# Interleaving two tensors: opening with one whole x tile and one whole y tile, in place of two halves of x

## The chip, the core and the metric

The kernel runs on one core of a Trainium2 chip. The metric is the device time of one execution in microseconds (us), as the median of several runs; smaller is better. Beside it stands the profile of one execution, taken by the hardware profiler, and its trace.

## What is computed

```python
def setup_inputs():
    batch, seq, dim = 32, 256, 1024
    # x and y: float32 of shape (batch, seq, dim)
...
def reference(x, y):
    result = np.zeros((batch, seq, dim * 2), dtype=np.float32)
    result[..., 0::2] = x
    result[..., 1::2] = y
    return result
```

The output takes its even elements from x and its odd ones from y. Nothing is calculated: each of the 33.55 MB inputs is read once, and 67.11 MB are written.

## The kernel before

The inputs are treated as flat arrays and cut into n = 8 tiles of 128 partitions by W = 8192 float32, 4 MB each. A partition's row of a tile is 32 KiB, and contiguous in memory. One x tile and one y tile make two output tiles of the same size: output half h of step k holds columns h x 4096 to (h + 1) x 4096 of both.

There are two buffers each for x (`xt`), y (`yt`) and the output (`ot`); step k uses `xt[k % 2]` and `yt[k % 2]`, and half h always uses `ot[h]`. The order is written by hand, with semaphores:

- **SyncE** issues the loads, x before y in each step (L45, L48). From step 2 on it waits until the buffer has been read: for x on the third copy of step k - 2, for y on the fourth (L43, L47; `woven` counts copies, four in a step).
- **VectorE** does the copies, four in a step: x into the even elements of half 0 (L60), y into its odd elements (L63), then the same two for half 1. Ahead of half 0 it waits for the step's x tile and, between the two copies, for its y tile (L55, L62). Ahead of each x copy from step 1 on it waits until the store that last read this output buffer has landed (L59).
- **ScalarE** issues the stores: one for each half, after the y copy of that half (L67, L68).

The first tile of x is different. It is loaded as two halves of 128 x 4096 (rows of 16 KiB), the first on SyncE's queue (L37), the second on ScalarE's (L38), each with its own semaphore; VectorE waits for the second half only ahead of its second x copy (L57). In step 0 SyncE's loop then loads only y (L44 to L48). After the kernel is written, lines 88 to 107 take the first DMA of SyncE and the first of ScalarE out of the body and put them in the opening block of the program, ahead of that engine's drain; both must be free of waits.

The kernel ends when ScalarE has seen the last stores of both halves land (L72 to L78).

Of the kernel before, what the change touches and what calls it, by code (L numbers as in the profile page):

```python
# [3 lines left out]


def _interleave(nc, x, y, out):
    P = 128
    W = 8192
    H = W // 2  # L10

    total = 1
    for s in x.shape:
        total *= s
    n = total // (P * W)
    assert n * P * W == total

    def rows(ap, names, k):
        flat = ap.rearrange("b s d -> (b s d)")
        return flat[k * names : (k + 1) * names].rearrange("(p w) -> p w", p=P)  # L20

    fp32 = mybir.dt.float32
    xt = [nc.alloc_sbuf_tensor(f"xt{b}", [P, W], fp32).ap() for b in (0, 1)]
    yt = [nc.alloc_sbuf_tensor(f"yt{b}", [P, W], fp32).ap() for b in (0, 1)]
    ot = [nc.alloc_sbuf_tensor(f"ot{b}", [P, W], fp32).ap() for b in (0, 1)]

    xsem = [nc.alloc_semaphore(f"xsem{b}") for b in (0, 1)]
    hsem = nc.alloc_semaphore("hsem")
    ysem = [nc.alloc_semaphore(f"ysem{b}") for b in (0, 1)]
    woven = nc.alloc_semaphore("woven")  # L30
    osem = [nc.alloc_semaphore(f"osem{b}") for b in (0, 1)]

    xs = [rows(x, P * W, k) for k in range(n)]
    ys = [rows(y, P * W, k) for k in range(n)]
    os_ = [rows(out, 2 * P * W, k) for k in range(n)]

    nc.sync.dma_start(out=xt[0][:, :H], in_=xs[0][:, :H]).then_inc(xsem[0], 16)  # L37
    nc.scalar.dma_start(out=xt[0][:, H:], in_=xs[0][:, H:]).then_inc(hsem, 16)  # L38

    for k in range(n):  # L40
        b = k % 2
        if k >= 2:
            nc.sync.wait_ge(woven, 4 * (k - 2) + 3)  # L43
        if k:  # L44
            nc.sync.dma_start(out=xt[b], in_=xs[k]).then_inc(xsem[b], 16)  # L45
        if k >= 2:
            nc.sync.wait_ge(woven, 4 * (k - 2) + 4)  # L47
        nc.sync.dma_start(out=yt[b], in_=ys[k]).then_inc(ysem[b], 16)  # L48

    for k in range(n):  # L50
        b = k % 2
        for h in (0, 1):
            c = slice(h * H, (h + 1) * H)
            if h == 0:
                nc.vector.wait_ge(xsem[b], 16 * (k // 2 + 1))  # L55
            elif k == 0:
                nc.vector.wait_ge(hsem, 16)  # L57
            if k:
                nc.vector.wait_ge(osem[h], 16 * k)  # L59
            nc.vector.tensor_copy(out=ot[h][:, 0::2], in_=xt[b][:, c]).then_inc(woven, 1)  # L60
            if h == 0:
                nc.vector.wait_ge(ysem[b], 16 * (k // 2 + 1))  # L62
            nc.vector.tensor_copy(out=ot[h][:, 1::2], in_=yt[b][:, c]).then_inc(woven, 1)  # L63

    for k in range(n):
        for h in (0, 1):
            nc.scalar.wait_ge(woven, 4 * k + 2 * h + 2)  # L67
            nc.scalar.dma_start(  # L68
                out=os_[k][:, h * W : (h + 1) * W], in_=ot[h]
            ).then_inc(osem[h], 16)  # L70

    nc.scalar.wait_ge(osem[0], 16 * n)  # L72
    used = sorted(s.num for s in [*xsem, hsem, *ysem, woven, osem[0]])
    assert used == list(range(used[0], used[-1] + 1)), used
    nc.scalar.sem_clear(range(used[0], used[-1] + 1))
    nc.scalar.nop(nofuse=True).wait_op(osem[1], 16 * n, "sem-ge").then_inc(
        osem[1], -16 * n
    )  # L78


def kernel(tc, x, y, out):
    nc = tc.nc
    tc.close()
    tc.compile()

    _interleave(nc, x, y, out)

    blocks = nc.main_func.blocks
    for engine in (mybir.EngineType.SP, mybir.EngineType.Activation):
        opening = blocks[0].instructions  # L90
        at, moved = next(
            (b, i)
            for b in blocks[1:]
            for i in b.instructions
            if i.engine == engine and i.opcode == "DMACopy"
        )
        assert not (moved.sync_info and moved.sync_info.on_wait)
        body = at.instructions
        body.remove(moved)
        gate = next(  # L100
            n
            for n, i in enumerate(opening)
            if i.engine == engine and i.opcode == "Drain"
        )
        opening.insert(gate, moved)
        at.instructions = body
        blocks[0].instructions = opening


# [1 line left out]
_INS = ['x', 'y']  # L111
_OUTS = [((32, 256, 2048), 'float32')]


# [23 lines left out]
```

## Time and profile before

| | |
|---|---|
| time, median of 5 runs | 314.73 us (314.59 to 314.93) |
| profiled execution, its own time | 314.71 us |
| its span | 313.2 us |
| VectorE busy | 72.6 us (23%), 32 copies of 2.29 us |
| DMA | 134.22 MB, mean 429 GB/s over the span, 4752 packets |
| SyncE's queue (q1) | 2304 packets, 65.01 MB |
| ScalarE's queue (q10) | 2448 packets, 69.21 MB |

The span runs from the first instruction recorded to the last event; the time of the execution lies 1.5 us above it. Part 2 of the page cuts the span in 40 slices of 7.8 us: each digit is the busy share in tenths, and for DMA the mean share of the core's 16 DMA engines. The answers by stretch give the same for any stretch asked for; DMA bytes and times are booked in the stretch where a packet starts, so short stretches can stand above the true rate and their neighbours below it. Transfers "to landing" are timed from the instruction that issues them to the last increment of their semaphore; in a queue with other transfers ahead, that holds their time in the queue.

### The profile page before, as it was taken

The page shows a single profiled execution, that of the slowest core. Times are in us where ns is not written, and L with a number is a line of the kernel's source. Part 1 is how long each engine was busy: PE and PEld are TensorE (multiplying, and loading weights), DVE is VectorE, ACT ScalarE, POOL GpSimd, SP SyncE. Part 2 cuts the span into 40 slices and gives each one's busy share as a digit, 9 for nine tenths or more (in the row PEclk, how much of TensorE's full clock was granted, in tenths as well). Part 3 has the DMA queues.
Part 4 walks back from the last instruction along what each step waited for, and adds up shares of the span by engine and source line. Part 5 has one row for each costly group of instructions (what it writes and reads, how often), then busy time and mean ns, then how long its engine had stood idle before and what let it go on. Part 6 is the DMA issues. An engine that isn't in the chain of part 4 may idle for free.

```text
span 313.2 us, 113 instructions
## 1 busy us (share of the span) xinstructions
DVE 72.6 (23%) x32; POOL 0.2 (0%) x4
## 2 busy tenths in 40 slices
DVE  0216002232022410324003250031501315013510
POOL 0000000000000000000000000000000000000000
DMA  8999999999999999999999999999999999999998
GB/s 343 460 410 393 444 427 431 439 427 444 418 452 410 460 402 469 402 465 406 456 414 444 427 431 439 427 444 418 452 410 460 402 469 402 465 406 456 414 444 360
DMA packets 4752, 134.22 MB, mean 429 GB/s; under 512 B 528, under 2 KB 528, under 8 KB 528
## 3 DMA queue, kind: packets, MB, share of 16 engines
q10 hardware_dynamic: 2448, 69.21, 51.2%
q1 hardware_dynamic: 2304, 65.01, 48.6%
HBM read 67.11 MB, written 67.11 MB: 429 GB/s over the span
## 4 chain that ended last, share of the span: by engine, by line
DMA 82%; DVE 12%; issue 0%
DMA out_dram<-ot 76%; DMA yt<-in_y_dram 6%; DVE ot L63 6%; DVE ot L60 6%
## 5 line engine op out<-in xcount | busy, mean ns | idle before, releaser
L60 DVE COPY ot<-xt 128x4096 f32<-128x4096 f32 x16 | 36.7, 2295 | 183.0 <-DMA out_dram<-ot 171.4
L63 DVE COPY ot<-yt 128x4096 f32<-128x4096 f32 x16 | 36.7, 2292 | 42.7 <-DMA yt<-in_y_dram 42.7
L122 POOL MEMSET const-bfloat16-1.0<- 128x1 bf16 x1 | 0.1, 102 | 0.0
L122 POOL MEMSET const-uint8-127<- 128x1 uint8 x1 | 0.1, 101 | 0.0
L122 POOL MEMSET const-float32-0.0<- 128x1 f32 x1 | 0.1, 99 | 0.2 <-issue 0.2
L122 POOL MEMSET const-float32-1.0<- 128x1 f32 x1 | 0.1, 98 | 0.0
## 6 DMA issues: line engine op xcount, KB each, us to landing
out_dram<-ot ACTq DMA_DIRECT2D x16, 4096.0 KB, 29.1
yt<-in_y_dram SPq DMA_DIRECT2D x8, 4096.0 KB, 60.8
xt<-in_x_dram SPq DMA_DIRECT2D x7, 4096.0 KB, 43.6
xt<-in_x_dram SPq DMA_DIRECT2D x1, 2048.0 KB, 11.6
xt<-in_x_dram ACTq DMA_DIRECT2D x1, 2048.0 KB, 13.3
```

What stands on the lines that cost most here:

```text
L60: nc.vector.tensor_copy(out=ot[h][:, 0::2], in_=xt[b][:, c]).then_inc(woven, 1)
L63: nc.vector.tensor_copy(out=ot[h][:, 1::2], in_=yt[b][:, c]).then_inc(woven, 1)
L122: nc = _bacc.Bacc("TRN2", target_bir_lowering=False, num_devices=1)
```

## The change

The first x tile is loaded whole by SyncE, and the first y tile whole by ScalarE, both in rows of 32 KiB. SyncE's loop then issues nothing in step 0. The semaphore of the second half of x, and VectorE's wait for it, are gone.

```diff
@@ -25,7 +25,6 @@
     xsem = [nc.alloc_semaphore(f"xsem{b}") for b in (0, 1)]
-    hsem = nc.alloc_semaphore("hsem")
     ysem = [nc.alloc_semaphore(f"ysem{b}") for b in (0, 1)]
...
-    nc.sync.dma_start(out=xt[0][:, :H], in_=xs[0][:, :H]).then_inc(xsem[0], 16)
-    nc.scalar.dma_start(out=xt[0][:, H:], in_=xs[0][:, H:]).then_inc(hsem, 16)
+    nc.sync.dma_start(out=xt[0], in_=xs[0]).then_inc(xsem[0], 16)
+    nc.scalar.dma_start(out=yt[0], in_=ys[0]).then_inc(ysem[0], 16)
 
     for k in range(n):
         b = k % 2
...
             nc.sync.dma_start(out=xt[b], in_=xs[k]).then_inc(xsem[b], 16)
         if k >= 2:
             nc.sync.wait_ge(woven, 4 * (k - 2) + 4)
-        nc.sync.dma_start(out=yt[b], in_=ys[k]).then_inc(ysem[b], 16)
+        if k:
+            nc.sync.dma_start(out=yt[b], in_=ys[k]).then_inc(ysem[b], 16)
 
     for k in range(n):
         b = k % 2
...
             if h == 0:
                 nc.vector.wait_ge(xsem[b], 16 * (k // 2 + 1))
-            elif k == 0:
-                nc.vector.wait_ge(hsem, 16)
             if k:
                 nc.vector.wait_ge(osem[h], 16 * k)
...
-    used = sorted(s.num for s in [*xsem, hsem, *ysem, woven, osem[0]])
+    used = sorted(s.num for s in [*xsem, *ysem, woven, osem[0]])
```

The program's order of instructions changes on two engines. SyncE has the x tile 0, then the x and y tiles 1, then those of step 2 behind their waits; it had half of x tile 0, y tile 0, x and y tile 1. ScalarE opens with y tile 0 and goes on with the 16 stores as before. VectorE's 32 copies keep their order.

## The prediction

> **What bounds the kernel now.** I read the page first, part 2, for whether any engine is full.
>
> ```profile
> DVE  0216002232022410324003250031501315013510
> ...
> DMA  8999999999999999999999999999999999999998
> GB/s 343 460 410 393 444 427 431 439 427 444 418 452 410 460 402 469 402 465 406 456 414 444 427 431 439 427 444 418 452 410 460 402 469 402 465 406 456 414 444 360
> ```
>
> VectorE is idle for most of every slice; the DMA engines are at 9 from the second slice to the last but one. The GB/s row swings because a transfer is booked where it starts, so I asked for wider stretches, with the opening cut fine. The columns are the stretch, its length, busy time of VectorE and GpSimd, clock, DMA share, GB/s.
>
> ```profile
> 0.00:4.00 4.00, 0.00 (x0) 0.20 (x4) 1.00 0.79 266
> 4.00:24.00 20.00, 4.35 (x2) 0.00 (x0) 1.00 1.03 445
> 24.00:32.00 8.00, 4.65 (x3) 0.00 (x0) 1.00 0.99 381
> 32.00:152.00 120.00, 27.27 (x12) 0.00 (x0) 1.00 1.00 433
> 152.00:272.00 120.00, 27.26 (x12) 0.00 (x0) 1.00 1.00 433
> ```
>
> Both long stretches move 433 GB/s at a share of 1.00. That is the ceiling of this kernel: 134.22 MB (part 2) / 433 GB/s = 310.0 us of the 313.2 us span. About 3.2 us are left for everything else: the start, the end, and whatever is lost on the way. By this view 0 to 4 us loses (433 - 266) x 4 / 433 = 1.5 us and 24 to 32 us loses (433 - 381) x 8 / 433 = 0.96 us. Stretch 4 to 24 shows 445, above the ceiling, by the same booking; so these two losses may each be off by some tenths.
>
> The chain that ended last, in its first 68 us, says which instructions set the opening (start, length, what):
>
> ```profile
> 1.57 20.36 DMA yt<-in_y_dram
> 21.93 0.02 issue
> 21.95 2.29 DVE ot L63
> 24.25 2.21 DVE ot L60
> 26.45 2.21 DVE ot L63
> 28.66 0.02 issue
> 28.68 38.84 DMA out_dram<-ot
> ```
>
> The chain looks serial, but its DMA links are elastic: the store issued at 28.68 takes 38.84 us, a 4 MB tile that at 433 GB/s needs 9.7. It is queued behind the store before it, and shares the engines with loads. So a chain that begins later gets shorter waits, as long as both queues hold work. **The question is therefore not whether the first store is late, but whether the DMA engines go idle.**
>
> **The change, part by part.** The bytes stay (the same tiles, loaded once), and so do the 32 copies and 16 stores. One DMA goes (33 to 32): two 2 MB halves of x and a y tile become one x tile and one y tile. By the order of instructions, SyncE then has x0, x1, y1 ahead of its first wait, where it had half of x0, y0, x1, y1; ScalarE opens with y0 where it had the other half of x0.
>
> 1. When x0 and y0 land. The issues of before:
>
> ```profile
> yt<-in_y_dram SPq DMA_DIRECT2D x8, 4096.0 KB, 60.8
> ...
> xt<-in_x_dram SPq DMA_DIRECT2D x1, 2048.0 KB, 11.6
> xt<-in_x_dram ACTq DMA_DIRECT2D x1, 2048.0 KB, 13.3
> ```
>
> The two halves, issued at 0.00 and 0.12, land at 11.6 and 0.12 + 13.3 = 13.4: together, so the two queues share the engines in small turns. From 13.4 to y0's landing at 21.93 (chain) are 8.5 us, at 433 GB/s 3.68 MB of y0's 4.19; the other 0.51 MB came before ScalarE's half was through. That is one 32 KiB row on each of 16 engines (0.52 MB): SyncE's queue got one row of its next tile in ahead of the end of ScalarE's transfer. In after the same happens with x1's first row: y0 lands when x0, y0 and one row per engine of x1 have moved, 0.52 MB / 433 = **1.2 us later**, at 23.1. Before, x0's first half led by 13.4 - 11.6 = 1.8 us (a half row, 0.6, and a whole one, 1.2); now it is two whole rows, so x0 lands at about 23.1 - 2.4 = 20.7, not 11.6.
>
> The Trainium skill (DMA: Bandwidth & Descriptors, Queues, rings and completion order) has each engine drain a packet of some 9 to 17 descriptors from one ring before it turns to the next. An engine's share of one of these DMAs is about that long, so by the rule x0 would drain whole, then y0 would land at 21.9 as before, and this step would cost 0. The landings 11.6 and 13.4 speak for the finer turns, and I go by them.
>
> 2. VectorE. The first copy (L60, 2.29 us) ran from 11.63, far ahead. With x0 at 20.7 it ends at 23.0, still before y0 at 23.1. So the early copy stays hidden under y0's transfer, by only 0.1 us; were that cover gone, the first store would slip by up to 2.3 us more. The copies after it follow as before: 2.3 us to the first store, now issued at 25.5 instead of 24.28; the second at 29.9 instead of 28.7; SyncE's x2 and y2, which wait for the third and fourth copy, at 27.7 and 29.9 instead of 26.48 and 28.68. No wait is added; the one on the second half of x0 goes.
>
> 3. Do the engines run dry meanwhile? Behind x0, SyncE's queue holds x1 and y1, 8.39 MB, 19.4 us of transfer at 433 GB/s. From 23.1 they last alone until over 40 us, and x2 is there by 27.7. So the 1.2 us are filled with loads that have to be done anyway. Cost 0; without that cover it would be 1.2 us. VectorE's waits then take up the shift: its longest, 19.6 us for the first store's landing, shows the room.
>
> 4. The middle and the end. The loads are ahead of the stores by about 0.5 MB more, so they are through a little sooner and the stores run alone a little longer. From 286 us on only stores are under way:
>
> ```profile
> 280.54 2.29 DVE L60 COPY ot<-xt 128x4096 f32<-128x4096 f32 x1 [14.88 <-DMA out_dram<-ot]
> 287.80 2.30 DVE L63 COPY ot<-yt 128x4096 f32<-128x4096 f32 x1 [4.96 <-DMA yt<-in_y_dram]
> 293.85 2.29 DVE L60 COPY ot<-xt 128x4096 f32<-128x4096 f32 x1 [3.75 <-DMA out_dram<-ot]
> 296.06 2.29 DVE L63 COPY ot<-yt 128x4096 f32<-128x4096 f32 x1
> ```
>
> The last store is issued at 298.4; the one before it takes 9.7 us from 293.8, to 303.5. So ScalarE's queue has 5 us in hand, and this doesn't depend on the shift. Cost 0.
>
> 5. Rows of 32 KiB in the opening. In the trace's records of single DMA packets, which no part of the page prints, a row of 16 KiB takes 611 ns and one of 32 KiB 1213. Per engine 16 half rows go for 8 whole: 16 x 611 - 8 x 1213 = 72 ns, plus one semaphore record of 9 ns: -0.1 us.
>
> 6. The cold start. No row shows a first transfer of 32 KiB rows. The first 16 KiB rows took 1.0 to 1.4 us, 0.4 to 0.8 over the 611. If that excess is a latency it stays (0); if it grows with the row it doubles (+0.6). Below nothing: were the excess gone, -0.6, but the first read has to come from somewhere, so I see no way. I take 0, as second rows are mostly at 611 already.
>
> The Trainium skill (DMA: Bandwidth & Descriptors, Latency and other measured facts) speaks against streams at large power-of-two distances in HBM: 512 KiB between rows gave 207 GB/s. If two tensors read side by side counted as such, an estimate by that figure is 8.39 MB / 207 - 8.39 / 433 = +21 us. The rows here lie 32 KiB apart as before, and the 433 of before comes with loads and stores on different tensors together, so I give it nothing.
>
> 7. The dip at 24 to 32 us. It begins with the first store. Should it come from the first store itself, it only moves by 1.2 us: 0. Should it come from ScalarE's queue starting anew after 11 us of rest (13.4 to 24.3), it may shrink, since the rest is now 23.1 to 25.5: down to -0.96. The first reason is nearer, as ScalarE's first load at 0.12 shows no dip of its own; I take 0.
>
> Sum against the profiled run (314.71 us, 1.5 outside its span; the median shown is 314.73): 314.71 - 0.1 = **314.6 us**.
>
> **The rivals.**
> - The shift is handed on (slower). The first store is 1.2 us late, and the chain runs from it through 15 stores to the end. If anywhere behind it the engines idle for want of a store or a load, the delay comes out whole: 314.7 + 1.2 = 315.9. It decides from the point where one queue is empty while the other's next transfer is still waited for. For it: the chain itself, 76% in stores. Against it: 433 GB/s at a share of 1.00 over 240 us, so there is no idle time of the engines that a delay could enter.
> - The dip goes (faster). ScalarE's queue is nearly in steady use, and the 0.96 us at 24 to 32 are not lost: 314.6 - 0.96 = 313.6. For it: the dip comes when that queue starts again. Against it: the first store after loads is as new as before.
> - The order is not shared but whole tiles (the change then moves almost nothing on the way to the first store): x0 at 11.6, y0 at 21.9, 314.6 as well.
>
> **How the numbers follow.** Forecast, full DMA engines hide the shift: 0.74, 314.1 (half the dip) to 315.3 (step 6 at +0.6, rounded). Whole tiles in turn: 0.03. Handed on: 0.15. Dip gone: 0.08. About 0.2% (0.63 us) is what a measurement of this kernel can tell from no change: faster 0.08, same 0.77, slower 0.15. The range takes in the slower rival and leaves out the faster: 314.0 to 315.9, some 9 in 10 by these cases, cut for sizes I don't foresee.
>
> **What would show it.** Right: the first L60 copy starting near 20.7, the first L63 copy near 23.1, the first store near 25.5; 433 GB/s from 32 us on; a stretch of 24 to 32 still below 400; first stretch near 266; the end of the span 1.5 us under the time. Wrong: a DMA share under 0.98 in any long stretch from 32 us on, the first 4 us under 230 GB/s (cold rows cost more), or no dip.

## The result and the profile after

| | before | after |
|---|---|---|
| median | 314.72 us (44 runs, 314.5 to 315.23) | 315.04 us (26 runs, 314.83 to 315.41) |
| profiled execution | 314.71 us | 315.41 us, the highest of its runs |
| its span | 313.2 us | 313.9 us |

The ratio is 1.0011, 95% interval 1.0006 to 1.0017. So the change lies within the 0.2% that the prediction called the same, and within its range, but it is slower by a small amount that is clear of noise, where the forecast had a gain of 0.1 us. What has to be explained is small: 0.3 us in the median, 0.7 us between the two traces.

The issue of the first store before, and then the first copies and the first store of after, in order of time (start, length, what; in brackets what ended the idle time before it; the length of a store's line covers several issues):

```profile
24.28 4.77 ACTq L68 DMA_DIRECT2D out_dram<-ot  x2
```

```profile
21.88 2.30 DVE L58 COPY ot<-xt 128x4096 f32<-128x4096 f32 x1 [21.88 <-DMA xt<-in_x_dram]
24.08 2.29 DVE L61 COPY ot<-yt 128x4096 f32<-128x4096 f32 x1
26.29 2.29 DVE L58 COPY ot<-xt 128x4096 f32<-128x4096 f32 x1
26.41 48.74 ACTq L66 DMA_DIRECT2D out_dram<-ot  x4
```

x0 lands at 21.85, not at 11.6 as its first half did; y0 at 22.0 (21.9 from its issue at 0.12), practically where it was (21.93). The first x copy is no longer hidden under y0's transfer, and the first store is issued 2.13 us later than before (24.28). The stretches of after, by the same cuts (stretch, length, busy time of VectorE and GpSimd, clock, DMA share, GB/s):

```profile
0.00:4.00 4.00, 0.00 (x0) 0.20 (x4) 1.00 0.75 270
4.00:24.00 20.00, 2.12 (x1) 0.00 (x0) 1.00 1.03 444
24.00:32.00 8.00, 6.78 (x4) 0.00 (x0) 1.00 0.99 365
32.00:152.00 120.00, 27.07 (x12) 0.00 (x0) 1.00 1.00 433
152.00:272.00 120.00, 27.47 (x13) 0.00 (x0) 1.00 1.00 433
```

Only the third line has moved: 365 where it was 381. (433 - 365) x 8 / 433 = 1.26 us are lost there, 0.3 more than before. From 32 us on the engines move 433 GB/s, as before, although everything is issued later; what takes up the delay is VectorE's waits (engine, line, what it waited for, us in total, times, longest):

```profile
DVE ot L58 <- DMA out_dram<-ot: 192.6, 14, 20.1
...
DVE ot L61 <- DMA yt<-in_y_dram: 12.1, 7, 1.7
```

Before, the second of these rows was

```profile
DVE ot L63 <- DMA yt<-in_y_dram: 42.7, 8, 8.0
```

The loads are now further ahead of the stores, so y is waited for less and the stores more.

What the 0.3 us do at the end is seen in the last microsecond. A packet is booked where it starts, so a stretch near the end tells how many engines still start a 32 KiB row there. Before and after:

```profile
311.70:312.00 0.30, 0.00 (x0) 0.00 (x0) 1.00 0.00 0
312.00:313.00 1.00, 0.00 (x0) 0.00 (x0) 1.00 0.01 0
```

```profile
311.70:312.00 0.30, 0.00 (x0) 0.00 (x0) 1.00 1.01 437
312.00:313.00 1.00, 0.00 (x0) 0.00 (x0) 1.00 0.08 33
```

Before, no engine starts a row after 311.7 us. After, four start one by 312.0 (437 GB/s x 0.3 us = 131 KB), and one engine alone starts one later (33 KB, one row). The kernel waits for all sixteen increments of the last store's semaphore, one from each engine, so it ends when the last of the 16 engines does.

The records of single packets, which no view prints whole, give the rest; I followed each engine as a chain of packets without gaps. Beyond the plain 611 ns and 1213 ns of a row, the engines lose 0.83 us each on average between 20 and 48 us before, and 1.17 after, and nothing after 48 us in either. The last increment of the last store's semaphore comes at 312.84 before and 313.54 after: 0.70 us later, as the two times are (315.41 - 314.71 = 0.70). The times of last increments are counted, here and below, from a zero that lies about 0.34 us behind that of the views, where the two are at 313.18 and 313.88; all other times are those of the views. And in both kernels the loss is where the first store's rows join the loads: it covers the two load rows per engine ahead of the first store row. Below, this is called the **join**; its stall is the average per engine from these records, of one trace for each kernel.

### The profile page after: what moved, and what is told of

Its sections match the earlier page's. It is cut to its first block, busy times and chain, and to the rows that moved or that the text cites. A ratio compares the mean times of both kernels' runs of the same rounds, so it can differ in the third digit from the quotient of the medians.

```text
span 313.9 us, 112 instructions
## 1 busy us (share of the span) xinstructions
DVE 72.5 (23%) x32; POOL 0.2 (0%) x4
## 4 chain that ended last, share of the span: by engine, by line
DMA 82%; DVE 13%; issue 0%
DMA out_dram<-ot 75%; DMA xt<-in_x_dram 7%; DVE ot L58 7%; DVE ot L61 6%
## 6 DMA issues: line engine op xcount, KB each, us to landing
yt<-in_y_dram ACTq DMA_DIRECT2D x1, 4096.0 KB, 21.9
```

## The experiments

**The theories.** All loss is at the join. Theory 1: it is larger because the first store comes later. Rival 1: the opening costs it, by its 32 KiB rows or its queues. Rival 2: it is what ScalarE's queue pays for starting anew, or what the output's first write pays; then it could be avoided.

**before_hold.** Only the moment of the first store is changed, in the kernel before:

```diff
             if k:
                 nc.vector.wait_ge(osem[h], 16 * k)
+            elif h == 0:
+                nc.vector.wait_ge(ysem[0], 16)
             nc.vector.tensor_copy(out=ot[h][:, 0::2], ...)
```

> The kernel before, with one more wait: the first x copy waits for the first y tile, so that the four copies of step 0 run in a row and the first store is issued near 26.4 us, as in the changed kernel, while the opening's loads stay as they were. Theory (the loss is the stall of the DMA engines around the first store, and it grows because this store comes 2.1 us later): the stall grows from 0.83 us per engine to about 1.2, time 315.0. Rival (the opening's queues or rows cost it, not the store's moment): 314.7, stall 0.8.

Measured: first store issued at 26.69 us; 315.51 us median (315.05 to 320.22), ratio 1.004 (1.0015 to 1.0064). So the opening of before is slow too when its first store comes where the changed kernel has it. But eight of the twelve runs lie at 315.05 to 315.52 and four at 318.05 to 320.22, which nothing here explains and which lift the ratio above that of the medians. The trace is of one of the two fastest runs (315.05). Its average stall did not grow (0.64, where the theory wanted 1.2); its last increment came late all the same (313.18), on one engine. So the moment of the store is borne out, and the larger average stall is not.

**after_rows16.** The changed kernel in 16 KiB rows:

```diff
-    nc.sync.dma_start(out=xt[0], in_=xs[0]).then_inc(xsem[0], 16)
-    nc.scalar.dma_start(out=yt[0], in_=ys[0]).then_inc(ysem[0], 16)
+    for c in (slice(0, H), slice(H, W)):
+        nc.sync.dma_start(out=xt[0][:, c], in_=xs[0][:, c]).then_inc(xsem[0], 16)
+        nc.scalar.dma_start(out=yt[0][:, c], in_=ys[0][:, c]).then_inc(ysem[0], 16)
```

> The changed kernel with both opening tiles cut in two DMAs of 16 KiB rows each, VectorE waiting for both halves as it waits for the whole. Theory (the moment of the first store): 315.0, stall near 1.2 us per engine. Rival (rows of 32 KiB in the opening): back to 314.7, stall near 0.8.

Measured: 314.70 us, ratio 0.9998 (0.9989 to 1.0006), stall 0.77. That is what the rival said. But the first store was issued at 25.96 here, 0.45 us earlier than in the changed kernel, so the run had not changed the rows alone. Theory 1 in its simple form (later is worse) has to explain why 1.7 us later than before costs nothing and 2.1 us costs 0.3. So the run leaves the rows of the opening open; the delayed stores below, which keep these rows, bear on them.

**y1_on_act and warm_out** try rival 2. The first adds `nc.scalar.dma_start(out=yt[1], in_=ys[1])` behind y0 and leaves y1 out of SyncE's loop; the second puts a 512-byte-per-row copy from x to the output ahead of y0 on ScalarE's queue.

> The changed kernel with the second y tile on ScalarE's queue too, behind the first, so that this queue is never empty when the first store joins it; the store then starts behind y1, near 40 us. If the stall comes from a queue that starts anew: it is gone, 314.0 or less. If it comes from the first store itself: it moves to about 40 us and stays near 1 us, 314.7 to 315.1. If the delay of the stores were handed on to the end: 10 us more.

Measured: 316.26 us, ratio 1.0047 (1.0035 to 1.0059). Its stretches:

```profile
36.00:44.00 8.00, 0.00 (x0) 0.00 (x0) 1.00 1.00 393
44.00:76.00 32.00, 4.50 (x2) 0.00 (x0) 1.00 0.99 426
76.00:84.00 8.00, 3.21 (x2) 0.00 (x0) 1.00 1.06 459
84.00:96.00 12.00, 1.66 (x2) 0.00 (x0) 1.00 0.98 371
96.00:272.00 176.00, 42.33 (x20) 0.00 (x0) 1.00 1.00 433
```

The store joins behind y1 on a queue that was never empty, and 36 to 44 us still dips to 393. A second dip follows at 84 to 96 (371, by the same sum 1.7 us): there SyncE's queue had run dry (no load row starts between 77.8 and 87.9 us), as x3 was issued late, at 83.11, and loads join stores that are alone. So the stall of the first store is not its queue's new start: in both dips transfers of the other direction join a stream of one direction, once stores join loads and once loads join stores.

> The changed kernel with a small copy from x to the output in HBM (512 bytes in each of 128 rows, overwritten by the first store later) as ScalarE's first DMA. If the stall is the first write to HBM or to the output: it goes, or moves into the first 3 us, where the engines wait anyway, 314.0 to 314.3. If it belongs to the store's read from SBUF or to the queue's new start: it stays near 1.2 us, 315.0 to 315.3.

Measured: 314.92 us, ratio 1.0005 (0.9996 to 1.0013). The dip stays (365 GB/s at 36 to 44 us, where this kernel's store joins, as y0 had been pushed behind a part of the loads; stall 0.95). A first small write to HBM doesn't take it away.

**The first store, moved in steps.** Copies of some columns of x into a spare tile, ahead of the first copy, delay the first store of the changed kernel and leave its opening as it is:

```diff
             if k:
                 nc.vector.wait_ge(osem[h], 16 * k)
+            elif h == 0:
+                nc.vector.tensor_copy(out=junk[:, 0::2], in_=xt[0][:, :512])
```

> The changed kernel with one more VectorE copy ahead of the first, of 512 columns of x into a spare tile (not part of the result), so that the first store is issued about 0.3 us later. Theory of the beat (each engine takes a row every 1.21 us; what the first store costs depends on where in this beat it arrives, because the engines take it in at different rows when it arrives at a row's edge): the time changes with the delay and comes back after 1.2 us, so that among delays of 0.3, 0.6, 0.9 and 1.2 us one or two lie at 314.7, with the sixteen landings of x1 within 0.5 us. Theory of lateness: it grows step by step, 315.1 here. Theory of the 32 KiB rows in the opening: all four at 315.0.

> As the run with 512 columns, with 1024 and a delay of about 0.6 us, half of the beat. Beat: 314.7. Lateness: 315.1. Rows of the opening: 315.0.

> As the run with 512 columns, with 1536 and a delay of about 0.9 us. Beat: 314.7 to 315.0. Lateness: 315.2. Rows of the opening: 315.0.

> As the run with 512 columns, with two copies of 1024 and a delay of about 1.2 us, one whole beat. Beat: as the changed kernel, 315.0. Lateness: 315.2. Rows of the opening: 315.0.

After these four, two more, one to the other side of the slow stretch and one in the kernel before (a copy of 512 columns ahead of its first y copy):

> The changed kernel with two more VectorE copies of 1536 columns each into a spare tile ahead of the first, so that the first store is issued about 1.8 us later, near 28.2 us; this is one beat of 1.21 us behind the run delayed by 0.6 us, which was the slowest. Theory of the beat: slow again, 315.4. Theory of the tile's edge (the first store costs more where it joins the loads at the end of one load tile and the start of the next, which is near its issue at 26.4 to 27.2 and over by 27.5): 314.7.

> The kernel before with one more VectorE copy of 512 columns of y into a spare tile ahead of the first y copy, so that the first store is issued near 24.6 us, two beats ahead of 27.0, where the slowest run had it. Beat: 315.4. Tile's edge (the store joins in the middle of x1's rows): 314.7.

All of them in order of the first store's issue:

| kernel | first store issued, us | median, us | ratio to before, interval | stall, us | last increment, us |
|---|---|---|---|---|---|
| before | 24.28 | 314.72 | | 0.83 | 312.84 |
| before_late512 | 24.60 | 314.63 | 0.9998 (0.9988 to 1.0007) | 0.72 | 312.69 |
| after_rows16 | 25.96 | 314.70 | 0.9998 (0.9989 to 1.0006) | 0.77 | 312.83 |
| after | 26.41 | 315.04 | 1.0011 (1.0006 to 1.0017) | 1.17 | 313.54 |
| after_late512 | 26.65 | 315.08 | 1.0014 (0.9997 to 1.0031) | 1.07 | 313.07 |
| before_hold | 26.69 | 315.51 | 1.004 (1.0015 to 1.0064) | 0.64 | 313.18 |
| after_late1024 | 27.00 | 315.44 | 1.0018 (1.0008 to 1.0029) | 1.18 | 313.58 |
| after_late1536 | 27.20 | 315.21 | 1.0011 (1.0002 to 1.002) | 1.34 | 313.32 |
| after_late2048 | 27.51 | 314.74 | 0.9997 (0.9988 to 1.0006) | 0.90 | 312.86 |
| after_late3072 | 28.09 | 315.94 | 1.0038 (1.0014 to 1.0061) | 0.83 | 312.79 |

The time is no rising function of the delay: theory 1 falls. With the opening of the changed kernel untouched it is back at 314.74 when the store is issued 1.1 us later, so its 32 KiB rows alone do not cost the 0.3 us. The theory of the beat (in the expectation of after_late512) wanted 314.7 of after_late1024, 315.0 of after_late2048 and 315.4 of before_late512, and none of the three came. What is left is a place: all issues from 26.4 to 27.2 have a higher median than before, whichever opening they have, though the interval of after_late512 takes in no change. Some 5.4 us after its issue the store's first rows start (31.8 us in after), and there tile x1's eight rows per engine, the first load behind the opening, come to their end and y1 begins. That is theory 2, the **tile's edge**. By the records the place is narrow: in after_rows16 the store joins one row ahead of x1's last (stall 0.77), in after_late2048 one row behind it on most engines (0.90). Theory 2 doesn't cover after_late3072 whole, which it expected at 314.7 and the beat at 315.4: its runs lie at 314.47 to 314.71, 315.65 to 315.96 and 316.95 to 317.51. The lowest group is as expected; the others, steps of about 1.2 us, are not explained.

The records show one more join at an edge: in warm_out the first store's rows start at 41.5 to 42.0 us, right behind y1's last load rows. Its stall is 0.95 and its median 314.92, above before's, with an interval that takes in no change. So a join at an edge does not always cost 0.3 us.

**before_cut96** meant to put an edge under the join of before: tile x1 in two DMAs of 96 and 32 partitions.

> The kernel before with x tile 1 loaded by two DMAs, of 96 and of 32 partitions, which are 6 and 2 rows for each engine; in the trace of before the first store joined behind the sixth row of x1. So an edge between two load DMAs is put where the first store joins, and nothing else is moved. Tile's edge: 315.0 to 315.4. Beat, or anything tied to the store's moment alone: 314.7.

Measured: 322.16 us, ratio 1.0231 (1.0216 to 1.0247). It tells nothing of the edge, since the DMA of 96 partitions was slow by itself, before the first store's rows started (31.0 us):

```profile
12.00:24.00 12.00, 3.57 (x2) 0.00 (x0) 1.00 1.08 393
24.00:32.00 8.00, 5.27 (x3) 0.00 (x0) 1.00 0.83 201
```

**rows16_early**: the opening's four halves with a semaphore each, so that the first store comes early, while 16 KiB rows are under way.

> The changed kernel with both opening tiles cut in halves of 16 KiB rows, x and y beside each other, and each half with a semaphore of its own, so that the first store is issued near 14 us, while 16 KiB rows are on the way. If the stall at the first store goes with the rows under way, it is halved, 0.4 us per engine, and the time is 314.3; if it is a fixed latency, 314.7.

Measured: 316.63 us, ratio 1.0052 (1.0031 to 1.0072). The stall at the join is 0.76 us per engine, not half: it doesn't go with the size of the rows. More is lost later: 414 GB/s at 64 to 72 us, where ScalarE's queue had run dry (no store row starts from 60.1 to 66.8 us) and stores join loads once more, and 399 at 288 to 300, where the loads end.

**after_mid_y1 and after_end_y1** are the test of theory 2, on another tile: five and ten copies of 1500 columns into the spare tile, one after the other, which move the join into the middle and to the end of y1.

> The changed kernel with five small copies into a spare tile ahead of the first copy, so that the first store is issued some 4.7 us later, near 31.1 us, and joins the loads near 36.4 us, in the middle of tile y1. Tile's edge: 314.7 with little spread. Lateness: above 315.4, the slowest so far. Chance: 314.7 to 315.4 with spread.

> As the run that joins in the middle of y1, with ten small copies: the first store is issued near 35.8 us, 4.8 us ahead of the end of tile y1, as in the changed kernel it is some 4.4 to 5 us ahead of the end of x1. Tile's edge: slow again, 315.0 to 315.5. Lateness: slower than the join in the middle of y1. If edges don't matter: as that run.

Measured: first store issued at 31.05 us, 314.83 us, ratio 1.0006 (0.9997 to 1.0016), stall 0.83, last increment 312.81; and issued at 36.06 us, 315.27 us, ratio 1.0018 (1.0008 to 1.0027), stall 1.02, last increment 313.19. So a join in the middle of a tile costs what it cost before, though it comes 6.8 us later, and one at the end of a tile is slow again. That is what theory 2 said; lateness would have had both slow, and the opening is the same in both. Here is how many rows of the store (q10) and of the loads (q1) start in a stretch around the join (queue: packets, MB, share). In the middle of y1, 34 to 36.5 us:

```profile
q1 hardware_dynamic: 15, 0.49, 56.0%
q10 hardware_dynamic: 7, 0.23, 21.2%
```

The engines part 7 to 9: seven take the store's first row in at once, the others one load row later, and this run is no slower than before. At the end of y1, 39.7 to 41.1 us, then after itself, 30 to 31.4 us, then before_hold, 29.8 to 31.2 us:

```profile
q10 hardware_dynamic: 1, 0.03, 5.4%
```

```profile
q1 hardware_dynamic: 2, 0.07, 18.4%
q10 hardware_dynamic: 1, 0.03, 5.4%
```

```profile
q1 hardware_dynamic: 11, 0.36, 86.8%
q10 hardware_dynamic: 1, 0.03, 5.4%
```

Here one engine alone takes a row of the store in first, ahead of the last row of the load tile, and the other fifteen after it. The records show this engine stalled twice, around that store row: some 1.6 us in all in after, where the others lose 1.1 on average, and some 1.3 in after_end_y1, against 1.0.

**after_again and after_late3072_again** are second traces.

> The changed kernel once more, for a second trace. If the time is made by the stall at the first store on the engine that leaves it last: the last increment of the last store lies about 1.9 us under the time again (313.5 for 315.4 in the first trace), and a faster run shows a smaller stall in the stretch from 24 to 36 us. If not: the stall is as before while the time differs.

Measured: 315.32 us, stall 1.18, last increment 313.44, again 1.9 us under the time, and again one engine ahead (30 to 31.4 us):

```profile
q1 hardware_dynamic: 8, 0.26, 70.3%
q10 hardware_dynamic: 1, 0.03, 5.4%
```

> The kernel with a delay of 1.8 us once more, whose runs lay at 314.5 to 314.7, 315.7 to 316.0 and 317.0 to 317.5, some 1.2 us apart, which is a 32 KiB row's time on one engine. If a slow one is met: an engine takes its turn of loads and stores otherwise than the others from the first store on and ends a row, or two, later. If a fast one: a stall near 0.8 us per engine as in its first trace.

Measured: 314.69 us, stall 0.89: a run of the lowest group once more, so what the other two groups do was not seen.

**after_quarter** moves the first store the other way, to the middle of x1: output half 0 of step 0 is made and stored in two pieces, the rest is the changed kernel.

```diff
+            if k == 0 and h == 0:
+                nc.vector.tensor_copy(out=ot[0][:, 0:H:2], in_=xt[0][:, :Q])
+                nc.vector.wait_ge(ysem[0], 16)
+                nc.vector.tensor_copy(out=ot[0][:, 1:H:2], in_=yt[0][:, :Q]).then_inc(quarter, 1)
...
+                nc.scalar.wait_ge(quarter, 1)
+                nc.scalar.dma_start(out=os_[0][:, :H], in_=ot[0][:, :H]).then_inc(osem[0], 16)
```

> The changed kernel, its opening untouched, with output half 0 of step 0 made and stored in two pieces of 4096 columns, so that the first store (of 16 KiB rows) is issued near 24.2 us, as in the kernel before, and joins the loads in the middle of tile x1. Tile's edge: 314.7, the stall near 0.8 us per engine and the last store's sixteen increments within 0.5 us. If the opening itself costs it: 315.0 or more.

Measured: first store issued at 24.17 us, 315.08 us (314.64 to 315.77), ratio 1.001 (1.0001 to 1.0019). The stall at the join is 0.69, as for a join in the middle of a tile, and fifteen last increments lie between 312.17 and 312.53, better than before; but the sixteenth comes at 313.67. That engine lost its time later, in load rows at 57, 96 and 116 us, 0.96 us in all. Why it did is not shown; the run also brought in stores of 16 KiB rows beside loads of 32 KiB. So the join did as theory 2 said and the time did not; the run can't clear the opening by its time.

## Why the prediction was right and wrong

- **The bound, and "the question is whether the DMA engines go idle": right.** 433 GB/s from 32 us on, before and after, with the first store 2.1 us late. The rival that hands the delay on, +1.2 us for 1.2, did not come; for a shift of 2.1 it would have been +2.1.
- **Step 1, when x0 and y0 land: the turns were right in kind, the count was wrong.** Predicted 20.7 and 23.1, measured 21.85 and 22.0. The two queues took rows by strict turns from the start: the first 32 KiB rows, from 1.0 us, took 1.3 to 1.9 us, and ScalarE's first rows start right behind them, from 2.8 us, so x0 and y0 ended together. The Trainium skill (DMA: Bandwidth & Descriptors, Queues, rings and completion order) has an engine drain a whole packet, typically of 9 to 17 descriptors, from one ring before it turns to the next. The prediction's estimate by that rule, x0 at 11.6, is not what this trace shows (21.85).
- **Step 2, VectorE: the cover of 0.1 us named there was gone.** x0's landing, not y0's, releases the first copy, and the store slips 2.13 us in place of 1.2, to 26.41 in place of 25.5. The text had the price, up to 2.3 us, and not the case.
- **Steps 3 and 4, hidden by loads, and the end: right.** By the records no row lost anything behind the join, in either trace.
- **Step 5, -0.1 us: not seen.** It is under what the join does from run to run.
- **Step 6, the cold start: right.** 270 GB/s in the first 4 us against 266; the first rows took 0.5 us more than the plain 1213 ns on average, where those of 16 KiB had taken 0.6 more than 611.
- **Step 7, "it only moves by 1.2 us: 0": the step that failed.** The text took the cost of the first store's dip as the same wherever it falls. It moved, and where it came to lie it cost more: 1.26 us by the stretches against 0.96, 1.17 per engine against 0.83, and more on one engine; the median is 0.32 us longer. Both ends that the prediction named for this step, nothing and a gain of 0.96, left out a loss. The 0.9 us that steps 1 and 2 had missed may be what carried the store there: the slow issues of the table begin at 26.4, the forecast had 25.5, and a store at 25.96 (after_rows16) cost nothing; but no run issued one at 25.5 with this opening. That the dip belongs to the first store itself and not to ScalarE's queue starting anew was right (y1_on_act).

What is shown: the loss is at the join, and the trace of after ends later by what its last engine loses. Where the join costs more is supported, and not proven: in the kernels made from the changed one the stall is 0.95 to 1.34 where the store joins at the end of x1 or y1, against 0.69 to 0.90 elsewhere, and the test that was set up for it (after_mid_y1 and after_end_y1) came out as theory 2 said. Against it stand the times of after_late3072 and after_quarter, and warm_out, an edge where the time is hardly longer. With the opening of before there is one join at an edge, before_hold: it is slower too, but its average stall is not larger (0.64). What is argued only: why. An edge brings the end of one DMA (in after, the records of x1's increments on fifteen engines at 33.0 to 33.6 us, behind the first store row) to the same moment as the change of direction; no run here parted the two. Open stays also what the slower groups of after_late3072 and before_hold are. And that the slow stretch of issues is one place and not several small ones rests on ten issue times.

No version was found that beats the kernel before by more than the measurement can tell; before_late512, at 0.9998 (0.9988 to 1.0007), is the same.

## What to carry to other kernels

Where the DMA engines are full from end to end, ask of a delay not how long it is but whether it empties the engines: here a first store 2.1 us later cost 0.3 us. What did cost were the moments where stores first join loads, 0.6 to 1.3 us per engine, or loads join stores, 1.7 us by the stretches of y1_on_act. A warm-up, a busy queue or smaller rows didn't take that away, so let it come once, keep both queues from running dry afterwards, and try a join in the middle of a transfer, which was cheaper here in most runs. This kernel ends with its slowest engine, so look at how many engines are still at work in the last microsecond and not at the mean rate alone.

## What the runs showed of the hardware that was not expected

- A DMA of 96 partitions with 32 KiB rows, alone on the engines, took about 2.3 us for a row (1.5 to 2.6) where one of 128 partitions takes 1.21: 201 GB/s between 24 and 32 us, and a kernel 7.4 us slower for one such DMA (before_cut96). Why is not shown.
- Once two queues were out of step on one engine they stayed so: the sixteen increments of each load lay within 0.5 us before, and within 2.2 us after, from the second tile to the last. In after fifteen of x1's come by 33.95 us and the sixteenth at 35.55 (times of the views), which fits the engine that took the store in early and is a turn behind in the loads that follow.
